# Three edits to a tuned decoder-layer kernel: gate products in runs of four, one projection norm moved a chunk later, one norm broadcast put behind products

## The chip, the cores and the metric

One core of one Trainium2 chip runs the whole layer. The metric is the device time of one execution in microseconds (us); the time of the kernel before is the median of three runs. One further execution was profiled, and every statement about single instructions comes from that one.

## The reference, cut to what matters

The reference is one layer of a hybrid causal decoder, in float32, for a prompt of 2048 tokens and 64 sample tokens (2112 columns in all), with 1024 model features:

```
h    = rmsnorm(x, g_pre_mix)
proj = h @ w_in                # attention q, k, v; GLA q, k, v, r; and a_lr, 16 columns
logf = log_sigmoid(a_lr @ w_a2 + b_a) / 16        # forget gate of the GLA heads
mixed = concat(attention, gated linear attention) @ w_o
x1   = x + rmsnorm(mixed, g_post_mix)
h2   = rmsnorm(x1, g_pre_ffn)
g, u = split(h2 @ w_up)
f    = (gelu(causal_conv3(g)) * u) @ w_down
y    = x1 + rmsnorm(f, g_post_ffn)
```

Every rmsnorm needs, per token, the sum of squares over the 1024 features, its inverse root, and a multiplication of the row by it.

## The kernel before, in words

**Layout.** Features lie on the 128 partitions in 8 tiles (KT = 8), tokens on the free axis. A float32 product is made of three products of rounded parts (high by high, high by low, low by high), so every operand is split into a high part (ScalarE copy, L70) and a low part (a subtraction on VectorE or GpSimd, L73).

**Stages.** `sweeps` makes the input projections chunk by chunk (512 tokens, 576 in the last chunk), first the GLA columns (`sweep_b`, chunks 0 to 3), then the attention columns (`sweep_a`). Attention follows. `tail` then works on four chunks of 528 tokens (H = 264, two halves): the output projection with `w_o` (`wo`, four chunks), and the feed-forward part (`ffn`, four chunks).

**Gate products.** `xhat("b", c)` (L205) loads the 8 input tiles of chunk c into buffers called `raw` (four of them, `rawb=4`), scales each on VectorE (L228), splits it, and multiplies it by the 16 padded-to-32 columns of `a_lr` (`walr`) on TensorE (L247). Each of these products has 32 output rows; product kk goes to the 32 partitions from 32 * (kk % 4) of the PSUM tile `plr`, so four neighbours go to four different column groups of the array. They were issued two at a time, whenever k is odd. A float32 product shows as two records in the trace. A `raw` buffer can be loaded again only when the product and the split that read it are done. The tiles of chunk c + 1 are prepared during the last blocks (`v`) of `sweep_b(c)`: one `next(xg)` per block.

**Norms in the tail.** `rms_bcast` (L116) sums the squares over the partitions with TensorE (`pn`, L126: five small products), takes the inverse root on VectorE and GpSimd (L105, then the power on GpSimd, L107), and after `gap` steps broadcasts the result with five TensorE transposes (`pb`, L143); ScalarE copies it out (L63). `pin=True` puts these TensorE instructions, in TensorE's own order, behind the last product issued so far (`self.after`, L287: an order edge without a semaphore).

`post(c)` (L447) turns the projection of chunk c into the residual stream: first norm; then for each of 8 tiles a scaling (L1459), the addition of x (L1460), the store of `x1` (L1462), and the sum of squares for the next norm (L1278); then the second norm, whose row goes to `rs2` (L1469). It is a generator: each `yield` is one step, and others call it between their products. In `tail` (L1313 to L1330) `post(c)` is stepped while `wo(c + 1)` runs: two steps per output tile for even chunks, three for odd. What is left after `wo(3)`, that is the end of `post(2)` and all of `post(3)`, is the chain `pend` (L1335), which `ffn(0)` steps.

**Feed-forward.** `ffn(c)` (L1618) goes through groups of 4, 4, 4, 4, 2 and 4 blocks of 128 hidden features. For each pair of blocks it runs `strassen` twice (gate half and up half): seven block products of 12 matmuls each (L1583), from four blocks by Strassen's scheme; after the products 1, 3, 5 and 7 one step of `pend` is taken (L1587), after the others one step of `xprep(c + 1)` (L1589). Then `down` (L1598) multiplies the group by `w_down` (L92, tiles `pfd`). Weights come through eight slots `ws`; in chunk 0 they are loaded raw, summed (L1549 to L1552) and split on VectorE and ScalarE (`wsrc`, L1540), and stored for the later chunks, which load four of each seven ready-made (L1558).

The right-hand operands of the seven products are 14 blocks (`xst`) made by `xprep` and loaded by `xload` (L1522) through GpSimd's own DMA queue, two loads of 264 KB per block: product 1 (and 4) reads blocks 0 to 3, product 2 (and 6) blocks 4 to 7, product 3 (and 5) blocks 8 to 11, product 7 blocks 12 and 13.

In `ffn(0)` the steps of `pend` that are left at the end of group 1 are run out (L1669); in the other chunks this happens at the end of group 0, and `pend` is then `final(c - 1)`, the last norm and store of the chunk before.

**Buffers.** `px` (L956) is one ring of four tiles of 264 KB: for x (`bx`), for `x1` in `final` (`fx`), and for the high parts in `xprep` (`xsh`). The projections `mot` of chunk 3 lie in the eight `acc` tiles (L1437) that `ffn(0)` uses for its sums after group 0.

**Order of the work.** The order on each engine and queue is set at build time: a list scheduler with a simulated timeline (`schedule_with_timeline_sim=True`, L1962) takes the instructions as the program issues them, and keeps the edges of `self.after`. Nothing around this change is ordered by hand but by these edges. Loads and stores go through SyncE's queue (SP) unless said otherwise; each queue is worked off in order.

## Time and profile before

| What | Value |
|---|---|
| Median of 3 runs | 2790.16 us (2789.48 to 2796.5) |
| The profiled execution's own time | 2790.49 us |
| Span of the profiled execution, first to last instruction | 2788.7 us |
| TensorE (PE) busy | 2680.4 us, 96% |
| VectorE (DVE) busy | 1829.6 us, 66% |
| ScalarE (ACT) busy | 1268.0 us, 45% |
| GpSimd (POOL) busy | 567.3 us, 20% |
| Mean granted TensorE clock | 0.979 of full speed |

The profile is one execution on the chip. "Busy" counts the time in which an engine has an instruction running; PEld is the load of weights into the array, which runs beside PE. In a table of windows, each row gives the stretch in us from the start of the span, its length, then for each engine the busy time and the number of its instructions in brackets, then the granted clock (PEclk, 1.00 is full speed), the busy share of the DMA engines and the GB/s that they moved. In a timeline, a row gives start, length, engine, line, operation, output and inputs, shape and count, and in brackets how long the engine had been idle and what ended this. In the chain that ended last, a row gives start, length, and the work that carried the chain. In a list of waits, the numbers are the sum in us, the number of waits and the longest.

### The profile page before, as it was taken

How to read it: one execution, taken by the hardware profiler on the slowest of the kernel's cores; microseconds unless marked ns; L12 is line 12 of the kernel's file. 1: busy time of each engine (PE TensorE's matmuls, PEld its weight loads, DVE VectorE, ACT ScalarE, POOL GpSimd, SP SyncE). 2: the span in 40 equal slices, each digit the busy share in tenths (PEclk: the TensorE clock that was granted, in tenths of full speed). 3: DMA queues.
4: the chain of work that ended last, by engine and by line, in shares of the span. 5: the costliest groups of instructions: out<-in, count | busy, mean ns of one | idle time of the engine just before them, and what ended most of it. 6: DMA issues, size and time to landing. Idle time of an engine off the chain costs nothing.

```text
span 2788.7 us, 58335 instructions
## 1 busy us (share of the span) xinstructions
PE 2680.4 (96%) x22203; PEld 2538.7 (91%) x22203; DVE 1829.6 (66%) x4508; ACT 1268.0 (45%) x2959; POOL 567.3 (20%) x626
## 2 busy tenths in 40 slices
PE   8999999999989898998999999999999999999998
PEld 6888899788778787998899999999999999999997
DVE  7557655454347577466989889676577765666666
ACT  6535433333257686344654444534244333443332
POOL 3434242443323567002000011000020000200001
PEclk9999999999999899999999999999999999999998
DMA  8755446789798855368578678886698865976654
GB/s 311 251 182 182 164 136 202 272 327 362 268 204 173 185 155 139 107 211 288 174 283 296 242 259 321 286 301 225 211 330 284 297 238 198 330 258 211 222 187 152
DMA packets 283591, 656.80 MB, mean 236 GB/s; under 512 B 31840, under 2 KB 81632, under 8 KB 281264
## 3 DMA queue, kind: packets, MB, share of 16 engines
q1 hardware_dynamic: 253008, 574.66, 61.2%
q0 software_dynamic: 13216, 46.56, 5.1%
q10 hardware_dynamic: 17088, 31.86, 3.2%
q8 instruction: 175, 2.87, 0.4%
q14 instruction: 104, 0.85, 0.1%
HBM read 509.02 MB, written 143.94 MB: 234 GB/s over the span
## 4 chain that ended last, share of the span: by engine, by line
PE 75%; DMA 9%; DVE 8%; POOL 3%; issue 3%; ACT 1%; SPq 1%; ACTq 0%; DVEq 0%; POOLq 0%
PE pfd L92 17%; PE pv L396 9%; PE pfa L1583 8%; PE pfe L1583 8%; PE pfd L1583 8%; PE pq L92 6%; PE pfb L1583 4%; PE pbo L1424 3%; PE pas L1815 2%; PE pao L1858 2%; PE pat L1841 1%; DVE ws L73 1%; DMA av<-out_o_vp 1%; DMA raw<-in_xp 1%; POOL aop L1222 1%
## 5 line engine op out<-in xcount | busy, mean ns | idle before, releaser
L70 ACT ACTIVATE ws<-wr 128x512 fp32r<-128x512 f32 (+1 forms) x482 | 293.3, 616 | 427.3 <-PE pfe L1583 142.6
L92 PE MATMUL pfd<-hh,ws 128*128 128x264 f32 x2816 | 475.8, 286 | 6.0 <-ACT ws L70 5.0
L92 PEld LDWEIGHTS pfd<-hh,ws 128*128 128x128 f32 x2816 | 401.5, 189 | 8.1 <-ACT ws L70 6.7
L73 DVE TENSOR_TENSOR ws<-wr,ws 128x512 fp32r<-128x512 f32 (+1 forms) x482 | 319.4, 668 | 128.1 <-ACT ws L70 124.1
L92 PE MATMUL pfd<-hl,ws 128*128 128x264 f32 x1408 | 303.5, 285 | 0.0
L1583 PE MATMUL pfa<-xh,ws 128*128 128x264 f32 x1496 | 292.0, 286 | 6.3 <-DVE ws L73 2.9
L1583 PE MATMUL pfe<-xh,ws 128*128 128x264 f32 x1496 | 289.2, 286 | 4.4 <-DVE u L1570 3.0
L1583 PE MATMUL pfd<-xh,ws 128*128 128x264 f32 x1408 | 288.5, 285 | 2.5 <-DVE up L1570 2.5
L1583 PEld LDWEIGHTS pfa<-xh,ws 128*128 128x128 f32 x1496 | 236.9, 190 | 7.8 <-DVE ws L73 3.3
L1583 PEld LDWEIGHTS pfe<-xh,ws 128*128 128x128 f32 x1496 | 236.1, 189 | 5.1 <-DVE u L1570 3.4
L396 PE MATMUL pv<-wh,xh 128*128 128x256 f32 (+1 forms) x816 | 235.2, 288 | 2.3 <-DVE th L693 2.3
L1583 PEld LDWEIGHTS pfd<-xh,ws 128*128 128x128 f32 x1408 | 231.0, 189 | 3.1 <-DVE up L1570 2.9
L396 PE MATMUL pv<-wh,xl 128*128 128x256 f32 (+1 forms) x816 | 233.1, 286 | 0.0
L396 PE MATMUL pv<-wl,xh 128*128 128x256 f32 (+1 forms) x816 | 232.9, 285 | 0.0
L92 PEld LDWEIGHTS pfd<-hl,ws 128*128 128x128 f32 x1408 | 226.5, 189 | 0.1
L1824 ACT ACTIVATE ass<-ass,aml 128x256 f32<-128x256 f32 (+1 forms) x384 | 173.5, 454 | 95.2 <-DVE aml L1820 94.4
L1532 POOL DMA_DIRECT2D xl<-d_xst x52 | 28.1, 540 | 904.5 <-PE pfe L1583 560.1
L1583 PE MATMUL pfd<-xl,ws 128*128 128x264 f32 x704 | 200.7, 285 | 0.0
L92 PE MATMUL pq<-xh,wh 128*128 128x512 f32 (+2 forms) x480 | 174.0, 370 | 10.1 <-ACT xh L234 7.7
L1583 PE MATMUL pfe<-xl,ws 128*128 128x264 f32 x616 | 175.6, 285 | 0.0
L1611 DVE TENSOR_TENSOR acc<-acc,pfd 128x264 f32<-128x264 f32 x304 | 116.2, 422 | 90.5 <-PE pfd L92 90.2
L92 PE MATMUL pq<-xl,wh 128*128 128x512 f32 (+2 forms) x480 | 175.1, 366 | 0.0
(334 smaller groups left out, 6645.2 us busy)
## 6 DMA issues: line engine op xcount, KB each, us to landing
ws<-d_wst SPq DMA_DIRECT2D x248, 512.0 KB
wr<-in_wu SPq DMA_DIRECT2D x114, 512.0 KB
d_wst<-ws SPq DMA_DIRECT2D x88, 512.0 KB
wr<-in_wd SPq DMA_DIRECT2D x160, 256.0 KB
wr<-in_wt SPq DMA_DIRECT2D x60, 512.0 KB
wh<-d_wbs SPq DMA_DIRECT2D x35, 512.0 KB
wl<-d_wbs SPq DMA_DIRECT2D x35, 512.0 KB
skp<-in_ckt SPq DMA_DIRECT2D x16, 1024.0 KB
```

Source lines behind the costliest of these rows:

```text
L70: h = nc.scalar.activation(hi, src, AF.Copy)
L73: return h, (nc.gpsimd if lo_eng == "p" else nc.vector).tensor_tensor(lo, src, hi.bitcast(F32), op=ALU.subtract)
L92: mm = nc.tensor.matmul(o, ww[:, k, :], xx[:, s0:s0 + n], start=(k == order[0] and i == 0), stop=(k == order[-1] and i == 2))
L396: mm = nc.tensor.matmul(ps[:m, :256], x[:, t0:t0 + m], w[:, k % 4, :], start=(k == 0 and i == 0), stop=(k == KT - 1 and i == 2))
L1222: line(nc.gpsimd.tensor_tensor(OP[i][:, :, sl], OP[i][:, :, sl], W[:, i], op=ALU.mult))
L1424: self.lastmm = nc.tensor.matmul(o, ww[:, k, :], xx[:, s0:s0 + n], start=k == self.WORD[0] and i == 0, stop=k == self.WORD[-1] and i == 2)
L1532: self.nc.gpsimd.dma_start(t.bitcast(F32), xo[i, z])
L1583: self.lastmm = nc.tensor.matmul(bank[:, :H], w[:, ww, k, :], xx, start=new and k == 0 and j == 0, stop=k == 3 and j == 2, skip_group_chec ...
L1611: nc.vector.tensor_tensor(acc[m][:, s0:s0 + n], acc[m][:, s0:s0 + n], pz, op=ALU.add)
L1815: self.line(nc.tensor.matmul(ps[:, sc:sc + nk], lq, rk[z], start=(z == 0), stop=(z == 1)))
L1824: ex = nc.scalar.activation(ssb[:, sc:sc + nk], ssb[:, sc:sc + nk], AF.Exp, bias=self.ml[:, idx, h:h + 1], scale=-1.0, accum_out=self.ml[: ...
L1858: self.line(nc.tensor.matmul(po[64 * h:64 * h + 64, blk, :], L.vq[self.base + kb][:, 64 * h:64 * h + 64], pt[:, j, :], start=st, stop=sp))
```

## The change

Three edits, which do not depend on each other:

1. `xhat`: the gate products are issued four at a time, at k = 3 and k = 7, each behind the one before (`self.after`), and, but for chunk 0, the first of a run behind the scaling of the fourth tile (`made`).
2. The norm of chunk 3's projection: `post(3)` is replaced by `post_norm(3)`, which takes the first norm only, stores the unscaled projection into `x1` and the norm's row into `rs2`; and by `post_late(3)`, which becomes `pend` of `ffn(1)` after its group 0. `post_late` loads the row, and for each tile the stored projection and x; it scales, adds, sums the squares, stores `x1` again; then it takes the second norm and stores `rs2` again. `ffn` gets a parameter `more` for it, and what is left of it is run out at the end of the last group.
3. The second norm of `post(2)` has a gap of 9 steps where it had 3. (The first norm of `post(3)` had a gap of 9 and its second one of 5; `post_norm(3)` has 4 and `post_late(3)` has a lead of 6 and a gap of 5.)

```diff
             else:
                 r = p.tile([128, self.W], F32, name=self.n("raw"), tag="raw", bufs=self.rawb)
                 nc.sync.dma_start(r[:, :w], self.a["xp" if ph == "a" else "xn"][:, k, c * 512:c * 512 + w])
-                nc.vector.scalar_tensor_tensor(r[:, :w], r[:, :w], self.gv[:, 0, k:k + 1], rb[:, :w],
-                                               op0=ALU.mult, op1=ALU.mult)
+                made = nc.vector.scalar_tensor_tensor(r[:, :w], r[:, :w], self.gv[:, 0, k:k + 1], rb[:, :w],
+                                                      op0=ALU.mult, op1=ALU.mult)
...
-                if k % 2:
+                if k % 4 == 3:
                     for z, n in ((0, 512), (1, w - 512)):
-                        for kk in (k - 1, k) if n else ():
+                        for kk in range(k - 3, k + 1) if n else ():
                             g = 32 * (kk % 4)
-                            nc.tensor.matmul(plr[g:g + 32, z, :n], walr[:, kk, :], rs[kk][:, 512 * z:512 * z + n],
-                                             start=(kk < 4), stop=(kk >= 4))
+                            mm = nc.tensor.matmul(plr[g:g + 32, z, :n], walr[:, kk, :], rs[kk][:, 512 * z:512 * z + n],
+                                                  start=(kk < 4), stop=(kk >= 4))
+                            if not first:
+                                self.after(mm, made)
+                            made = mm
...
-                    posts.append(self.post(c, self.mot, self.ssq))
+                    posts.append(self.post(c, self.mot, self.ssq) if c < 3 else self.post_norm(c, self.mot, self.ssq))
...
             for c in range(4):
-                pend = self.ffn(c, self.xnext, pend)
+                pend = self.ffn(c, self.xnext, pend, self.post_late(3) if c == 1 else None)
...
-        yield from self.rms(ssq, w, rb, 1, 3 if c < 3 else 9, pin=True)
+        yield from self.rms(ssq, w, rb, 1, 3, pin=True)
...
-        yield from self.rms(ssq2, w, rb2, 2, 3 if c < 3 else 5, pin=True)
+        yield from self.rms(ssq2, w, rb2, 2, 3 if c < 2 else 9, pin=True)
...
+    def post_norm(self, c, mot, ssq):
+        t0 = FCH[c][0]
+        w = 2 * H
+        rb = self.t528("brb", "rb", 2)
+        g = self.rms(ssq, w, rb, 1, 4, pin=True)
+        for m in range(KT):
+            self.nc.sync.dma_start(self.a["x1"][:, m, t0:t0 + w], mot[m])
+            if m % 2:
+                next(g, None)
+                yield
+        for _ in g:
+            yield
+        self.nc.sync.dma_start(self.a["rs2"][:, t0:t0 + w], rb)
+        yield
+
+    def post_late(self, c):
+        nc, a = self.nc, self.a
+        t0 = FCH[c][0]
+        w = 2 * H
+        rb = self.t528("brb", "rb", 2)
+        nc.sync.dma_start(rb, a["rs2"][:, t0:t0 + w])
+        ssq = self.t528("bssq2", "ssq", 2)
+        for m in range(KT):
+            r, o = self.px("bx"), self.px("bo")
+            nc.sync.dma_start(o, a["x1"][:, m, t0:t0 + w])
+            nc.sync.dma_start(r, a["xn"][:, m, t0:t0 + w])
+            yield
+            nc.vector.scalar_tensor_tensor(o, o, self.gv[:, 1, m:m + 1], rb, op0=ALU.mult, op1=ALU.mult)
+            nc.vector.tensor_tensor(o, r, o, op=ALU.add)
+            self.ssq_add(ssq, o, w, m == 0, "v")
+            nc.sync.dma_start(a["x1"][:, m, t0:t0 + w], o)
+            yield
+        rb2 = self.t528("brb", "rb", 2)
+        yield from self.rms(ssq, w, rb2, 6, 5, pin=True)
+        yield
+        nc.sync.dma_start(a["rs2"][:, t0:t0 + w], rb2)
+        yield
...
-            if gi == (c == 0) and pend is not None:
+            last = gi == len(FG) - 1
+            if (last or gi == (c == 0)) and pend is not None:
                 for _ in pend:
                     pass
-                pend = None
-            last = gi == len(FG) - 1
+                pend, more = more, None
```

2 lines of the change are left out of this document (1 added, 1 removed).

## The prediction

> **What bounds the kernel now.** I read the engines' table first, then windows of 50 us over the whole span, then narrower windows, the chain that ended last, and timelines where TensorE falls short.
>
> ```profile
> PE 2680.4 (96%) x22203; PEld 2538.7 (91%) x22203; DVE 1829.6 (66%) x4508; ACT 1268.0 (45%) x2959; POOL 567.3 (20%) x626
> ...
> 1300.00:1350.00 50.00, 40.41 (x316) 40.33 (x315) 40.22 (x80) 26.73 (x51) 9.23 (x12) 0.86 0.49 184
> 1350.00:1400.00 50.00, 43.49 (x316) 42.54 (x315) 47.81 (x90) 28.68 (x56) 0.00 (x0) 0.90 0.68 239
> 1500.00:1550.00 50.00, 47.26 (x383) 46.63 (x383) 45.88 (x94) 24.19 (x44) 0.00 (x0) 1.00 0.81 292
> 1550.00:1600.00 50.00, 50.00 (x415) 50.00 (x414) 44.39 (x91) 26.02 (x45) 0.00 (x0) 1.00 0.60 209
> ```
>
> TensorE is the bound: 96% busy. So an edit pays in two ways only: it makes TensorE's own work shorter, or it removes a stretch in which TensorE falls short. A full window of the feed-forward part holds 415 products of the array in 50 us, 0.1205 us each (1550 to 1600). The two windows after 1300 us, which are the first group of `ffn(0)`, hold 316 each: 99 too few, 12 us each, 24 us together. That is what edits 2 and 3 can work for. It is more than the idle time (9.6 and 6.5 us), because the granted clock fell as well. The narrow windows show two separate holes:
>
> ```profile
> 1304.00:1312.00 8.00, 0.00 (x0) 0.00 (x0) 7.35 (x14) 2.85 (x6) 5.51 (x7) 0.53 1.04 401
> 1312.00:1320.00 8.00, 7.54 (x42) 7.54 (x43) 0.88 (x2) 2.39 (x5) 0.41 (x1) 0.62 0.63 242
> 1344.00:1352.00 8.00, 8.00 (x69) 8.00 (x68) 8.00 (x14) 3.63 (x8) 0.00 (x0) 1.00 0.12 35
> 1352.00:1360.00 8.00, 6.07 (x50) 5.86 (x50) 8.00 (x17) 5.42 (x9) 0.00 (x0) 1.00 0.45 139
> 1360.00:1368.00 8.00, 6.06 (x42) 5.84 (x41) 8.00 (x16) 2.81 (x5) 0.00 (x0) 0.87 1.00 356
> 1368.00:1376.00 8.00, 5.36 (x27) 4.84 (x27) 8.00 (x17) 4.77 (x8) 0.00 (x0) 0.71 0.87 316
> 1376.00:1384.00 8.00, 8.00 (x54) 8.00 (x54) 8.00 (x17) 3.82 (x7) 0.00 (x0) 0.78 0.52 170
> ```
>
> **Edit 3, the broadcast of chunk 2's second norm.** The first hole is one instruction:
>
> ```profile
> 1301.70 1.17 PE L126 MATMUL pn<-c_ones,bssq 128*128 128x1 f32 x10
> ...
> 1309.71 2.71 POOL rcy L107
> 1312.46 1.33 PE pb L143 x5
> 1313.79 2.64 PE pfa L1583 x12
> 1316.43 2.24 PE pfb L1583 x12
> ...
> 1331.48 1.47 PE pfe L1583 x12
> ```
> ```profile
> PE pb L143 <- POOL rcy L107: 9.6, 1, 9.6
> ```
>
> The five transposes `pb` stand ahead of the first product in TensorE's order and wait for GpSimd's power, and GpSimd gets to it only at 1309.71, when it has issued its last load of `xst` blocks. TensorE stands for 9.6 us; then the clock is down, and the first two products take 2.64 and 2.24 us where one takes 1.47 later: 1.9 us more. At stake: 11.5 us.
>
> Counting the steps of `post(2)`, 20 are taken when `wo(3)` ends; with a gap of 9 the transposes come at the 25th. That is the fifth step that `ffn(0)` takes, behind the first strassen and one product more: eight products or so, 12 us. GpSimd's result is there at 1312.4, so it hides behind them. What is late next? Product 3, which reads blocks 8 to 11:
>
> ```profile
> 1296.64 0.54 POOL L1532 DMA_DIRECT2D xh<-d_xst  x1
> ...
> 1304.99 0.54 POOL L1532 DMA_DIRECT2D xl<-d_xst  x1
> ...
> 1297.74 0.44 SPq L1457 DMA_DIRECT2D bx<-in_xn  x1
> ...
> xl<-d_xst POOLq DMA_DIRECT2D x10, 264.0 KB, 7.3
> ...
> 1286.14 0.68 DVE L73 TENSOR_TENSOR ws<-wr,ws 128x512 fp32r<-128x512 f32 x1
> ...
> 1310.67 0.68 DVE L73 TENSOR_TENSOR ws<-wt,ws 128x512 fp32r<-128x512 f32 x1
> ...
> 1319.08 0.69 DVE L1549 TENSOR_TENSOR wt<-wr,wr 128x512 f32<-128x512 f32 x1 [7.73 <-DMA wr<-in_wu]
> ```
>
> The two loads of each block are issued in the order of the blocks; those of block 7 end at 1296.64, those of block 11 at 1304.99, and a load lands about 7.3 us later: 1303.9 and 1312.3. So products 1 and 2, whose split weights were ready by 1286.9, can run from 1302.9 to 1305.8, and product 3 waits until about 1312.3. Of the 11.5 us, 6.5 us of waiting come back, and some of the slow clock. But the four loads of x that `post(3)` makes ahead into the `px` ring go (the last at 1297.74; 1.06 MB, 2.6 us at the 401 GB/s of the window), so the blocks land earlier; and VectorE, which filled the eight weight slots by 1311.4 and then stood 7.7 us, can go on sooner. I take 5.5 us gained; the ends are 1, if weights are late as well, and 11.5, if nothing else is.
>
> **Edit 2 in `ffn(0)`.** In the second hole VectorE is busy 8.00 of 8.00 us in each row from 1344 to 1384. Full rows hold 69; the four after 1352 hold 173 instead of 276, which is 103 x 0.116 = 11.9 us. The work of `post(3)` in that stretch:
>
> ```profile
> L1459 DVE SCALAR_TENSOR_TENSOR bmo<-bmo,c_gvec,brb 128x528 f32<-128x528 f32 x8 | 5.5, 758 | 0.0
> L1460 DVE TENSOR_TENSOR bmo<-bx,bmo 128x528 f32<-128x528 f32 x8 | 5.5, 697 | 0.0
> ...
> L1278 DVE TENSOR_TENSOR bssq<-bssq,sq 128x528 f32<-128x528 f32 x7 | 4.9, 695 | 0.0
> ```
>
> It is 15.9 us of VectorE, more than the hole, and all of it leaves. What is late next is VectorE's other work (sums and splits of weights, evacuations), which fills about 85% of what remains; at such a load the window from 1500 to 1550 (45.88 of 50) still loses 3.9 us, the one from 1550 to 1600 (44.39) nothing. I keep 2 us of loss: 10 us gained, between 6 and 12. What `post_norm` leaves here costs TensorE nothing new: ten records `pn` and five transposes, as before, with GpSimd free of loads by then; the eight stores of `x1` wait only for ScalarE's copies and release the `acc` tiles sooner than the stores after scaling did.
>
> By the Trainium skill (TensorE: Matmul & The Clock Gate, "HAM oscillation"), only idle gaps over about 3.4 us lower the clock. By that rule the second hole, whose rows are idle for 1.9, 1.9 and 2.6 us of 8, would cost its idle 6.5 us alone, and edit 2 would gain about 5 us less. The trace disagrees: the clock went to 0.71 there.
>
> **Edit 1, the gate products.**
>
> ```profile
> 84.00:110.00 26.00, 4.38 (x16) 0.71 (x16) 1.00 0.73 256
> 180.00:206.00 26.00, 5.25 (x16) 0.71 (x16) 1.00 0.67 232
> 276.00:300.00 24.00, 5.69 (x32) 1.63 (x32) 1.00 0.74 262
> ```
> ```profile
> 18.62 1.92 PE L247 MATMUL plr<-raw,walr 128*32 128x512 f32 x16
> ...
> 95.68 1.05 PE L247 MATMUL plr<-raw,g_walr 128*32 128x512 f32 x4
> ...
> 100.87 1.23 PE L247 MATMUL plr<-raw,g_walr 128*32 128x512 f32 x6
> ...
> 107.48 1.04 PE L247 MATMUL plr<-raw,g_walr 128*32 128x512 f32 x2
> ...
> 278.32 1.16 PE L247 MATMUL plr<-raw,g_walr 128*32 128x512 f32 x8
> ```
>
> The windows count this line alone: chunks 1, 2 and 3 spend 15.3 us of TensorE on it. One product (x2) takes 1.04 us, two (x4) 1.05, three (x6) 1.23, all eight in chunk 0 (x16) 1.92: neighbours in different column groups overlap. A run of four is not shown; it lies between 1.05 and 1.92, nearest to the run of three, so I take 1.25, and 1.45 in chunk 3, whose last 64 columns add four short products (two of them made 1.05 into 1.16). Six runs: 4 x 1.25 + 2 x 1.45 = 7.9 us, a saving of 7.4; with 1.92 each it is 3.8. The Trainium skill (TensorEngine Tiling (Array Packing), "Key Properties") says that different tiles run in parallel: then a run of four would cost what one product costs, and the saving would be about 9 us. The run of three at 1.23 says that it is a little less.
>
> Against it: four `raw` buffers are now held until the fourth product, so tiles 4 to 7 can all be loaded only after the first run, where tiles 4 and 5 came earlier.
>
> ```profile
> 104.49 0.75 DVE L228 SCALAR_TENSOR_TENSOR raw<-raw,c_gvec,rb 128x512 f32<-128x512 f32 x1 [1.09 <-DMA raw<-in_xn]
> ```
>
> Tile 7 of chunk 1 was scaled at 104.49 after waiting for its load, and its gate product came at 107.48. TensorE now comes some 2 us sooner and tile 7 does not, and it still has to be split: I charge 0.8 us per chunk, 2.4 in all, and keep 5.0 us gained, between 0 and 8. Chunk 0 has all eight in one stretch already: nothing.
>
> **Edit 2 in `ffn(1)`.** `post_late` adds there what left `ffn(0)`, and eight stores and eight loads that did not exist.
>
> ```profile
> 1780.00:1870.00 90.00, 90.00 (x741) 90.00 (x741) 66.60 (x139) 37.77 (x68) 0.00 (x0) 1.00 0.86 307
> ...
> SPq L1462 <- DVE gt L1570: 12.8, 2, 12.6
> ```
>
> VectorE: 8 x (0.76 + 0.70 + 0.70) = 17.3 us on top of 66.6 in 90 us of groups 1 and 2: 93%. DMA: 24 transfers of 264 KB and two rows, 6.9 MB, 76 GB/s on top of 307: 383, under the 401 of the first hole. The norm's `pn` and `pb` have 10 products and more between them and GpSimd is free. TensorE has no idle time here, so nothing can be gained. The cost lies between 0 (like 1550 to 1600) and 7 us (3.9 us per 50, as in 1500 to 1550); I take 2.
>
> **The sum.** 5.5 + 10 + 5 - 2 = 18.5 us off the profiled execution's 2790.5 us (its span is 2788.7): 2772.0. The median of the runs shown, 2790.16, is the same within 0.4, so I predict 2772 for the median.
>
> **The rivals.** *The first hole stays.* Product 3 waits for its blocks, the clock falls, and by 1320 TensorE is where it was: for it, the loads go on until 1312 to 1316 and the DMA engines are full (share 1.04); against it, two products are surely done earlier. Then 10 + 5 - 2 = 13: 2777.5. *The holes close wholly.* The scheduler puts ready products of the up half into the wait: 10 + 11 + 7 - 1 = 27: 2763.5. *The late tiles eat edit 1.* If tile 7 comes 2.5 us late in each of three chunks, the 7.4 us are gone: 13.5, 2777. *The edges don't hold what they say*, since a list scheduler reorders everything and other stretches shift by chance: half of it, 2781. *Slower: SP's queue.* `post_late` takes two of four `px` tiles per step, `xprep(2)` uses the same ring, and a load that waits for a tile holds every weight load behind it on SP. The profile has such a hold: 12.6 us at a store of `x1` (L1462). The eight weight slots cover 8 x 1.47 = 11.8 us; a hold of 14.1 us in each of eight steps loses the whole gain of edits 1 to 3 (8 x 2.3 = 18.5), and 16 us gives 8 x 4.2 = 34, less 20.5: 2804. Against it: the ring turns in `final(0)` without such holds, and the scheduler places a load where it expects the tile to be free.
>
> **How the numbers follow.** Forecast 0.55 (its own range 2765 to 2779), first hole stays 0.13, holes close 0.12, late tiles 0.08, edges 0.07, slower 0.05. The unknown costs reach from 6 + 1 + 0 - 4 = 3 to 12 + 11.5 + 8 = 31; cut to eight cases in ten: 2762 to 2783. A difference of 0.3%, 8.4 us, is about what a measurement of this kernel can tell from no change. Faster by more than that (under 2781.8): 0.85; within it: 0.10; slower: 0.05.
>
> **What would show it.** Right: no idle time ahead of `pb` near 1302 us, product 1 starting within 1 us of `pn`, an idle of a few us ahead of product 3 named after an `xh` or `xl` load; between 1340 and 1384 rows with 66 or more products and VectorE under 7 of 8; six runs of gate products of 1.2 to 1.5 us after chunk 0; full windows in `ffn(1)` with VectorE near 40 of 50. The first group of `ffn(0)` should end near 1354 us instead of 1374. Wrong: `pb` or another norm still waiting for GpSimd; TensorE in `ffn(1)` waiting for `ws` loads or for VectorE by more than 7 us; TensorE waiting for `xh` or `xl` splits at the start of chunks 1 to 3.

## The result, and the profile after

Timed beside the kernel before on the same chip, the changed kernel takes 2780.7 us in the median of 8 runs (2776.14 to 2786.49), the kernel before 2793.42 us (8 runs, 2788.44 to 2800.43). The ratio is 0.9956, with a 95% interval of 0.9944 to 0.9968. On the 2790.16 us of the prediction that is 2777.9 us, with 2774.5 and 2781.2 as ends: faster by 12.3 us where 18.5 were forecast, inside the range. The profiled execution took 2780.57 us, with a span of 2778.5 us, 10.2 us less than the span before.

The table of engines, then windows of 50 us (start and end, length, busy time and count for each engine, clock, DMA share, GB/s), after the change. Line numbers from here on are the changed kernel's: the products of `strassen` are L1624, VectorE's evacuations L1611.

```profile
PE 2669.0 (96%) x22203; PEld 2530.5 (91%) x22203; DVE 1827.3 (66%) x4508; ACT 1271.4 (46%) x2961; POOL 568.2 (20%) x626
```
```profile
1300.00:1350.00 50.00, 44.65 (x344) 43.88 (x343) 45.11 (x89) 29.39 (x52) 3.41 (x3) 0.93 0.48 170
1350.00:1400.00 50.00, 50.00 (x412) 50.00 (x412) 40.33 (x76) 27.72 (x57) 0.00 (x0) 1.00 0.69 244
1500.00:1550.00 50.00, 50.00 (x412) 50.00 (x411) 45.86 (x92) 26.27 (x46) 0.00 (x0) 1.00 0.67 236
1550.00:1600.00 50.00, 50.00 (x414) 50.00 (x413) 40.41 (x84) 22.53 (x41) 0.00 (x0) 1.00 0.56 196
1780.00:1870.00 90.00, 89.09 (x731) 88.69 (x730) 70.79 (x150) 39.50 (x74) 1.56 (x1) 1.00 0.93 338
```

The two windows after 1300 held 316 products each; they hold 344 and 412. The window of `ffn(1)` held 741 and holds 731: something was paid there. The narrow rows and TensorE's waits between 1290 and 1330 show what became of the two holes.

```profile
1312.00:1320.00 8.00, 3.88 (x32) 3.66 (x30) 8.00 (x17) 6.19 (x10) 0.00 (x0) 0.95 0.37 112
1320.00:1328.00 8.00, 7.03 (x40) 7.03 (x41) 6.91 (x14) 2.55 (x4) 0.00 (x0) 0.63 0.28 97
...
1344.00:1352.00 8.00, 8.00 (x67) 8.00 (x67) 6.21 (x12) 3.95 (x8) 0.00 (x0) 1.00 0.82 301
1352.00:1360.00 8.00, 8.00 (x68) 8.00 (x67) 6.96 (x15) 4.54 (x9) 0.00 (x0) 1.00 0.66 194
1360.00:1368.00 8.00, 8.00 (x68) 8.00 (x67) 6.34 (x12) 5.87 (x13) 0.00 (x0) 1.00 0.64 211
```
```profile
1294.94 1.17 PE L126 MATMUL pn<-c_ones,bssq 128*128 128x1 f32 x10
1295.97 1.71 PE L1624 MATMUL pfa<-xh,ws 128*128 128x264 f32 x12
...
1299.68 0.52 PE L1624 MATMUL pfe<-xh,ws 128*128 128x264 f32 x2 [0.55 <-ACT ws L70]
...
1300.15 1.62 PE L1624 MATMUL pfa<-xh,ws 128*128 128x264 f32 x12
...
1302.22 0.28 PE L1624 MATMUL pfa<-xh,ws 128*128 128x264 f32 x1
```
```profile
PE pfe L1624 <- DVE u L1611: 5.4, 2, 5.1
```
```profile
1319.12 0.36 ACT L1615 COPY u<-pfa 128x264 f32<-128x264 f32 x1
```

The wait of `pb` is gone: the first product starts right behind `pn`. Behind products 1 and 2 (`pfa`, `pfb`) TensorE waits 0.55 us at the start of product 4 (`pfe`, which reads blocks 0 to 3), for ScalarE's split of its weights and not for blocks of x. Product 3 does not come next: the scheduler put product 1 of the up half (`pfa`, 1300.15) ahead of it, and product 3 (`pfa` from 1302.22, between pieces of products 4 and 5) waits for nothing. The second hole is gone altogether. But a new wait of 5.1 us stands in the first group, up to 1320.97, for an evacuation `u` that VectorE has to do; VectorE is busy 8.00 of 8.00 us in that row, so it lies behind other work in VectorE's queue, and the clock is at 0.63 in the row after. One input of that evacuation was late as well: ScalarE's copy of the up half's product 3 (the last row) ended at 1319.48. VectorE's queue alone accounts for the 1.0 us from there to 1320.50, where the evacuation starts.

The gate products (L247 alone) after the change, by window and as rows of the timeline:

```profile
84.00:110.00 26.00, 2.75 (x16) 0.45 (x16) 1.00 0.76 259
180.00:206.00 26.00, 2.79 (x16) 0.45 (x16) 1.00 0.68 229
274.00:300.00 26.00, 3.39 (x32) 0.94 (x32) 1.00 0.62 215
```
```profile
92.75 1.06 PE L247 MATMUL plr<-raw,g_walr 128*32 128x512 f32 x8
...
104.61 1.69 PE L247 MATMUL plr<-raw,g_walr 128*32 128x512 f32 x8
```
```profile
104.44 0.75 DVE L228 SCALAR_TENSOR_TENSOR raw<-raw,c_gvec,rb 128x512 f32<-128x512 f32 x1 [1.11 <-DMA raw<-in_xn]
```

15.3 us of TensorE have become 8.9. In the second run of chunk 1 three products start within 0.02 us and the fourth 0.64 us later, at 105.25, when VectorE's scaling of its tile (the last row), which had waited for a load, has ended; in chunk 2 it is 0.68 us.

**Where the time went, by stages.** All traces hold the same TensorE instructions apart from those of the norms (`pn`, `pb`), which the change moves. Without these each trace has 21957, so the time at which the Nth of them starts can be compared from kernel to kernel. Each number below is the us between two such starts, read from the traces of all thirteen kernels and of the kernel before; the experiments are described in the next section.

```
TensorE instruction    0-380 -1700 -2760 -10305 -11000 -11850 -13450 -16250 -21900  end
                       start  GLA1  GLA2  attn   ffn0a  ffn0b  ffn0c   ffn1   rest  
before                  76.1 175.9 123.4  922.0  113.1  109.4  200.3  347.8  697.6 23.2
gap_only                77.6 175.8 124.8  923.4   99.8  119.7  201.7  348.8  697.9 23.9
norm_only               73.9 176.0 121.8  919.1  101.3  110.7  200.2  356.3  700.0 23.8
no_gates                74.4 175.9 121.8  924.7   97.0  108.2  201.0  354.5  698.1 23.7
gates_only              77.1 174.3 125.5  916.9  110.8  110.2  200.5  349.7  698.1 22.9
after                   74.3 174.6 124.7  916.9   97.5  113.4  199.7  356.3  698.1 23.0
gates_422               76.3 177.5 122.2  918.7   97.7  108.7  201.1  355.8  699.8 23.2
no_late                 76.6 173.5 125.2  916.8   99.1  110.0  201.0  350.5  697.8 23.5
late_ahead              75.8 173.8 125.3  919.6   97.2  108.5  199.2  353.9  700.1 23.4
late_g3                 76.8 173.2 125.9  916.8   97.8  111.0  200.2  353.4  698.9 23.5
store_shift             73.9 173.6 125.7  919.2   98.3  110.0  199.7  362.9  697.9 23.8
xa_behind               74.4 172.9 123.0  917.5   98.3  111.6  200.8  357.6  699.4 23.3
late_g3_xa              76.9 173.1 123.4  918.8   96.7  112.0  200.5  353.0  698.0 22.8
all_three               73.9 173.4 123.2  917.3   97.3  110.0  201.5  362.3  698.5 23.1
```

GLA1 is the linear attention up to the middle of its last chunk but one, GLA2 the rest of it; "attn" is everything from there to the end of `wo`; ffn0a holds both holes. After less before, column by column and rounded at the end: -1.7, -1.2, +1.3, -5.1, -15.6, +4.0, -0.6, +8.5, +0.5, -0.2, together -10.2. The start (0 to 380) lies between 73.9 and 77.6 us over kernels that share its code, so its -1.7 is nothing. The rest has four parts: the two feed-forward holes gave 15.6; the gate products gave nothing inside the linear attention; 5.1 came from a stage that the diff does not touch; and 12.5 were paid back, in ffn0b and `ffn(1)`. There is one trace of each kernel, and a single column is no safer than this: in "attn" norm_only and no_gates have the same instructions in the same order on every engine and on SP, and take 919.1 and 924.7 us. The traced execution of gap_only is 8.9 us above that kernel's median; the others lie within about 4 us of theirs.

### The profile page after: what moved, and what is told of

It is laid out like the page before. It is cut to its first block, busy times and chain, and to the rows that moved or that the text cites. A ratio compares the mean times of both kernels' runs of the same rounds, so it can differ in the third digit from the quotient of the medians.

```text
span 2778.5 us, 58351 instructions
## 1 busy us (share of the span) xinstructions
PE 2669.0 (96%) x22203; PEld 2530.5 (91%) x22203; DVE 1827.3 (66%) x4508; ACT 1271.4 (46%) x2961; POOL 568.2 (20%) x626
## 4 chain that ended last, share of the span: by engine, by line
PE 78%; DMA 9%; DVE 6%; POOL 2%; issue 2%; ACT 2%; SPq 0%; ACTq 0%; DVEq 0%; POOLq 0%
PE pfd L92 17%; PE pv L399 9%; PE pfe L1624 8%; PE pfd L1624 8%; PE pfa L1624 8%; PE pbo L1427 7%; PE pq L92 6%; PE pfb L1624 4%; PE pas L1856 2%; DMA av<-out_o_vp 2%; DMA ws<-d_wst 2%; PE pao L1899 1%; PE pat L1882 1%; DMA raw<-in_xp 1%; DMA akl<-d_kl 1%
## 5 line engine op out<-in xcount | busy, mean ns | idle before, releaser
L1624 PE MATMUL pfe<-xh,ws 128*128 128x264 f32 x1496 | 291.5, 287 | 9.5 <-DVE u L1611 5.9
L1624 PE MATMUL pfa<-xh,ws 128*128 128x264 f32 x1496 | 290.0, 285 | 4.6 <-ACT ws L70 1.9
L1624 PE MATMUL pfd<-xh,ws 128*128 128x264 f32 x1408 | 290.8, 286 | 1.8 <-DMA ws<-d_wst 1.0
L1624 PEld LDWEIGHTS pfe<-xh,ws 128*128 128x128 f32 x1496 | 237.4, 190 | 11.3 <-DVE u L1611 7.0
L1624 PEld LDWEIGHTS pfa<-xh,ws 128*128 128x128 f32 x1496 | 235.3, 188 | 5.9 <-ACT ws L70 2.4
L1624 PEld LDWEIGHTS pfd<-xh,ws 128*128 128x128 f32 x1408 | 232.5, 190 | 2.6 <-DVE ws L73 1.4
L1624 PE MATMUL pfd<-xl,ws 128*128 128x264 f32 x704 | 201.2, 286 | 0.0
L92 PE MATMUL pq<-xh,wh 128*128 128x512 f32 (+2 forms) x480 | 171.3, 366 | 10.3 <-ACT xh L234 7.8
L1624 PE MATMUL pfe<-xl,ws 128*128 128x264 f32 x616 | 176.3, 286 | 0.0
L1624 PE MATMUL pfa<-xl,ws 128*128 128x264 f32 x616 | 174.9, 284 | 0.0
```

What stands on the lines that cost most here:

```text
L92: mm = nc.tensor.matmul(o, ww[:, k, :], xx[:, s0:s0 + n], start=(k == order[0] and i == 0), stop=(k == order[-1] and i == 2))
L1624: self.lastmm = nc.tensor.matmul(bank[:, :H], w[:, ww, k, :], xx, start=new and k == 0 and j == 0, stop=k == 3 and j == 2, skip_group_chec ...
```

## The experiments

My theories, the last of them formed after the first eight runs: (a) edit 1's saving is lost where the last chunk's decay runs, because four held `raw` buffers put late loads ahead of it in VectorE's queue; (b) the moved norm costs `ffn(1)` more than 2 us because its steps wait in in-order queues there; (c) the rest of the repayment is traffic on full DMA engines. Rivals: (a') the wait for `gS` comes from the decay's own length; (b') the work costs the same anywhere; (c') the queues and engines, not the traffic.

### The parts alone

**gates_only**, edit 1 alone on the kernel before:

```diff
-                if k % 2:
+                if k % 4 == 3:
...
-                        for kk in (k - 1, k) if n else ():
+                        for kk in range(k - 3, k + 1) if n else ():
...
+                            if not first:
+                                self.after(mm, made)
...
```


> Edit 1 alone: gate products in runs of four, everything else as before. In the profile of the changed kernel the gate products take 8.9 us of TensorE instead of 15.3, but at the end of the GLA stage only 1.7 us are left of these 6.4. Theory: in each chunk TensorE gets to the state products pgo earlier and waits there for VectorE's state update gS, which is queued behind the decay chain; the chain's end is set by loads into the raw buffers, which are now held until the fourth product. It expects 1 to 3 us faster than before (ratio 0.9990 to 0.9996), and in the trace the same wait of about 4 us of pgo for gS in chunk 3. Rival: the gain is real and was lost elsewhere in the changed kernel by chance of the schedule; it expects 5 to 6.4 us faster (ratio near 0.998).

Measured: 2788.83 us (12 runs, 2779.88 to 2802.4), before 2794.04 (25 runs); ratio 0.9983 (0.9969 to 0.9998). That is 4.7 us (0.6 to 8.6), nearer to the rival than to the theory, but the interval holds both. The trace has what the theory says: the linear attention is no shorter than before (299.7 us against 299.2), and `pgo` waits 4.2 us for `gS` in chunk 3.

**gap_only**, edit 3 alone:

```diff
-        yield from self.rms(ssq2, w, rb2, 2, 3 if c < 3 else 5, pin=True)
+        yield from self.rms(ssq2, w, rb2, 2, (3, 3, 9, 5)[c], pin=True)
```


> Edit 3 alone: the third chunk's second norm has a gap of 9 steps, the last chunk's norm stays where it was. Theory A, separate holes: the wait of 9.6 us for GpSimd goes, a shorter wait for VectorE or for loaded blocks comes, 3 to 6 us faster (ratio about 0.9985). Theory B, VectorE's work is what ends the first group of the first feed-forward chunk: TensorE runs ahead, meets the full VectorE earlier, and the second hole grows by what the first lost: within 2 us of before.

Measured: 2786.42 us (12 runs, 2778.69 to 2798.98); ratio 0.9979 (0.9964 to 0.9994): 5.9 us, the size of theory A. The trace, below, has theory B's second hole.

**norm_only**, edit 2 alone:

```diff
-                    posts.append(self.post(c, self.mot, self.ssq))
+                    posts.append(self.post(c, self.mot, self.ssq) if c < 3 else self.post_norm(c, self.mot, self.ssq))
...
-                pend = self.ffn(c, self.xnext, pend)
+                pend = self.ffn(c, self.xnext, pend, self.post_late(3) if c == 1 else None)
```


> Edit 2 alone: chunk 3's projection norm moved into the second feed-forward chunk; the gap of the third chunk's second norm stays at 3, so its broadcast stands ahead of the first product. Theory A, two separate holes: the second hole (about 12 us, VectorE full with the moved work) closes and the first (9.6 us of waiting for GpSimd) stays, less 4 to 7 us that the second chunk and the end of the first give back: 4 to 8 us faster, ratio about 0.998. Theory B, the two holes are one, because VectorE's work is what ends the first group: without edit 3 VectorE stands still while TensorE waits, and edit 2 alone still gains nearly all: 9 to 11 us faster.

Measured: 2783.29 us (7 runs, 2777.31 to 2786.94); ratio 0.996 (0.9946 to 0.9974): 11.2 us, the size of theory B. Its trace has theory A's mechanism: the first hole stays in full, and the second all but goes (TensorE is busy for 38.8 of the 40 us from 1340).

```profile
PE pb L143 <- POOL rcy L107: 9.6, 1, 9.6
```

**no_gates**, edits 2 and 3 without edit 1:

```diff
-                if k % 4 == 3:
+                if k % 2:
...
```


> Edits 2 and 3 without edit 1: the gate products again in pairs, the norm moved and the broadcast put back as in the changed kernel. Theory (the edits do not depend on each other, and edit 1 is worth 1.7 us): 8.5 to 11 us faster than before, ratio about 0.9965, and both holes after the end of the output projection closed as in the changed kernel: 14 us gained by the end of the first group of the first feed-forward chunk, and 5 to 7 us given back afterwards. Rival (edit 1 carries most of the measured gain, also through the attention, where the changed kernel's trace is 5 us shorter without any change of the program): 4 to 6 us faster.

Measured: 2779.85 us (6 runs, 2777.13 to 2788.28); ratio 0.9952 (0.9934 to 0.997): 13.4 us, more than both forecasts name, though the interval reaches down to 8.4. 16.1 us go out of ffn0a, where 14 were expected, and 6.2 come back by the end of `ffn(1)`, as expected.

What follows. The ratios of the single parts add up to more than the whole (4.7, 5.9 and 11.2 us against 12.3), each known to about 4 us; by stages, edits 2 and 3 give more together than apart. In its trace edit 3 alone takes 13.3 us out of ffn0a and gives 10.3 back in ffn0b: windows of gap_only show the second hole, only later.

```profile
1406.00:1416.00 10.00, 7.39 (x61) 7.18 (x59) 10.00 (x19) 6.00 (x13) 0.00 (x0) 1.00 0.97 352
1416.00:1426.00 10.00, 7.50 (x42) 7.51 (x43) 9.80 (x21) 4.59 (x8) 0.00 (x0) 0.66 0.74 282
```

VectorE is full there (10.00 and 9.80 of 10) with `post(3)`, which is still in its way. Edit 2 alone takes 11.8 out of ffn0a and returns 1.3; both together 16.1 and nothing returned. So edit 2 carries the gain of the first feed-forward chunk, and edit 3 adds 6.8 us to it over the two columns, where alone it keeps 3.0. And no_gates, without edit 1, is as fast as the whole change.

### What became of edit 1

In the columns GLA1 and GLA2 the kernels with runs of four and the decay's order as written (gates_only, after, no_late, late_ahead, late_g3, store_shift) take 173.8 and 125.4 us in the mean, the four without edit 1 take 175.9 and 122.9: 2.1 us gained, then 2.4 lost. The products of chunks 1 and 2 save 4.1 us, so half of that is gone within GLA1: TensorE's waits for VectorE from 72 to 252 us sum up to 3.6 us before and 7.0 after. The last chunk shows where the rest goes. TensorE's waits from 300 to 335 us, before and after:

```profile
PE pgo L827 <- DVE gS L836: 2.7, 1, 2.7
```
```profile
PE pgo L843 <- DVE gS L839: 4.0, 1, 4.0
```

TensorE comes earlier and waits longer for `gS`. VectorE's timeline after the change, on the way to it, with the product that the decay needs from TensorE and the loads from SP:

```profile
301.04 1.88 PE L630 MATMUL pz<-lr,g_wa 128*128 128x512 f32 x4
```
```profile
297.91 1.28 SPq L227 DMA_DIRECT2D raw<-in_xp  x3
```
```profile
302.74 1.55 DVE L228 SCALAR_TENSOR_TENSOR raw<-raw,c_gvec,rbp 128x576 f32<-128x576 f32 x2 [7.46 <-DMA raw<-in_xp]
...
305.72 1.40 DVE L631 TENSOR_SCALAR lfm<-pz,g_ba 128x512 f32<-128x512 f32 x2
...
313.16 0.34 DVE L632 SCALAR_TENSOR_TENSOR gB<-lfm,pz 128x64 f32<-128x64 f32 x2
```

VectorE stood idle for 7.5 us at the first scaling of the next phase's blocks, which waited for a load. SP issued that at 297.91, at the end of the second run of four, which held the buffers; before the change the first two went out at 292.68:

```profile
292.68 1.30 SPq L227 DMA_DIRECT2D raw<-in_xp  x2
```

`lfm`, whose products on TensorE began at 301.04, comes behind these scalings in VectorE's queue, at 305.72. The kernel before has scalings ahead of `lfm` too, with 2.9 and 1.0 us of waiting for loads, but there `lfm` starts 0.6 us after its product is done (304.23 after 303.68), and here 3.7 us (305.72 after 302.06).

**xa_behind**: the same kernel, with these scalings put behind the decay.

```diff
+                if ph == "a" and c == 3:
+                    self.after(made, self.lastdec)
...
-                nc.vector.scalar_tensor_tensor(t[:, sl], m[:, sl], 2.0, pzz, op0=ALU.mult, op1=ALU.subtract)
+                self.lastdec = nc.vector.scalar_tensor_tensor(t[:, sl], m[:, sl], 2.0, pzz, op0=ALU.mult, op1=ALU.subtract)
```


> The changed kernel with one order added: in the last chunk of the linear attention, VectorE's first touches of the next phase's input blocks come behind the last step of the decay (gB from pz). Theory: edit 1's saving is given back in the last chunk because the raw blocks held for the runs of four load late and stand ahead of the decay in VectorE's in-order queue; then the decay's lfm, which came 2.8 us after its product was done, comes 3 to 4 us earlier, PE's wait of 4.0 us for gS falls below 1.5 us, the linear attention ends 2 to 4 us earlier than in the changed kernel, and the whole is 2 to 4 us below it (about 2777.5). Rival: gS is late for another reason (the decay's own length, the PE work that now arrives sooner): the wait stays within 1 us of 4.0, and the time is the changed kernel's within 1.5 us.

```profile
300.48 0.75 DVE L633 TENSOR_SCALAR lfm<-pz,g_ba 128x512 f32<-128x512 f32 x1 [6.78 <-PE pz L632]
...
306.74 0.22 DVE L634 SCALAR_TENSOR_TENSOR gB<-lfm,pz 128x64 f32<-128x64 f32 x1
306.88 4.17 DVE L228 SCALAR_TENSOR_TENSOR raw<-raw,c_gvec,rbp 128x576 f32<-128x576 f32 x4
```

Measured: `lfm` comes 5.2 us and the last `gB` 6.4 us earlier (1.6 us of that is an earlier arrival at the stage), and the idle time ahead of `lfm` is now ended by TensorE (`pz`). The wait of 4.0 us is two of 2.3 and 1.4, in sum as long as the rival has it. GLA2 takes 123.0 us instead of 124.7, and the whole linear attention (380 to 2760) 295.9, 296.5 and 296.6 us in the three kernels with this order, against 298.8 to 299.7 in the six without it: 2.9 us in the mean, where 2 to 4 were expected. 2.2 of them lie in GLA2, which comes to 123.2 us in the mean, near the 122.9 of the kernels without edit 1. So theory (a) holds for the loss in the last chunk. No run has this order without edit 1, so how much the order alone would win there is open. The whole takes 2781.25 us (6 runs), ratio 0.9958 (0.9941 to 0.9974): nothing of it is left at the end, against what I expected.

**gates_422**: the last four products of a chunk in two runs of two.

```diff
-                if k % 4 == 3:
+                if k in (3, 5, 7):
...
-                        for kk in range(k - 3, k + 1) if n else ():
+                        for kk in range(0 if k == 3 else k - 1, k + 1) if n else ():
```


> The changed kernel with gate products in runs of four, two and two per chunk instead of four and four. Theory: holding four blocks until the last run delays the next loads; with the last four released two by two the loads of the last chunk's next phase issue about 3 to 5 us earlier, the wait for gS shrinks by 1 to 2 us, against about 1 us more per chunk for one run more on TensorE (gate products 8.9 to about 12 us in the three chunks): the linear attention ends within 1 us of the changed kernel's and the whole is the same within 1.5 us. Rival: the runs' cost alone decides, and it ends 2 to 3 us later.

Measured: 2783.45 us (6 runs), ratio 0.9966 (0.9952 to 0.9979). The gate products of chunks 1 to 3 take 15.6 us, as much as before: behind the first run of four they ran one at a time (in chunk 1 at 99.67, 100.72, 107.64 and 109.28), where I had expected two runs of two and about 12 us. GLA1 takes 177.5 and GLA2 122.2, 299.6 together, as in the changed kernel (299.3): the buffers come free earlier, the wait falls to 1.5 us, and the products' own time eats that. By the stage the theory's end holds; by the whole, 2.8 us above the changed kernel, its rival, but the two intervals overlap.

**What edit 1 did elsewhere.** The column "attn" is 916.8 to 919.6 us in the ten kernels with any form of edit 1 (mean 917.9) and 919.1 to 924.7 in the four without it (mean 922.3): 4.4 us, in a stage for which the diff has no line. The order of the instructions differs there all the same: between the kernel before and gates_only, 81 places of 7620 on TensorE (the first at 952 us), 54 of 1563 on VectorE and 44 of 1268 on ScalarE hold another instruction, while gap_only's order is the same as before's. So edit 1 shifts the order that the list scheduler chooses much later. That this order is the cause of the 4.4 us is not shown. Single executions of one order differ as much: norm_only and no_gates by 5.6 us over the stage, and gap_only spends 34.1 us between instructions 7260 and 7510 (919 to 945 us in the kernel before) where before spends 26.2.

### The moved norm in `ffn(1)`

**no_late**: `post_late` not run.

```diff
-                pend = self.ffn(c, self.xnext, pend, self.post_late(3) if c == 1 else None)
+                pend = self.ffn(c, self.xnext, pend, None)
```


> The changed kernel without the part of edit 2 that runs in the second feed-forward chunk: the last chunk's second norm is left out (its x1 stays unscaled, without the residual, and its rs2 is the first norm's). Theory: the moved steps cost 4 to 7 us there, since their loads and stores stand in queues that the down weights and the products' sums use; without them the wait for weights of about 4.6 us near the start of the steps goes, and the whole is 4 to 7 us below the changed kernel (about 2775). Rival: those waits are the round trips of weights that the kernel before has there too; then no more than 1.5 us is gained.

Measured: 2775.3 us (6 runs, 2774.0 to 2781.97), ratio 0.994 (0.9927 to 0.9952). `ffn(1)` takes 350.5 us instead of 356.3: the moved steps cost 5.8 us, sure to about 2 us, since the four other kernels with the same steps in this place (norm_only, no_gates, gates_422 and xa_behind) take 354.5 to 357.6. 1.9 of the 5.8 us are the norm's own products on TensorE:

```profile
1832.50 1.17 PE L126 MATMUL pn<-c_ones,bssq 128*128 128x1 f32 x10
...
1847.05 0.71 PE L143 MATMUL pb<-c_ident,rcy 128*128 128x128 f32 x5
```

The size is the theory's, the place is not: the wait near 1712 to 1742 stays. Windows of no_late, then of the changed kernel:

```profile
1712.00:1742.00 30.00, 24.51 (x181) 23.50 (x179) 25.69 (x51) 12.10 (x21) 0.00 (x0) 0.94 0.80 264
```
```profile
1712.00:1742.00 30.00, 24.08 (x164) 22.81 (x164) 24.71 (x48) 10.40 (x18) 0.00 (x0) 0.89 0.84 296
1742.00:1832.00 90.00, 90.00 (x741) 90.00 (x740) 71.08 (x145) 44.04 (x87) 0.00 (x0) 1.00 0.90 331
1832.00:1877.00 45.00, 44.09 (x362) 43.69 (x361) 33.95 (x71) 19.86 (x38) 1.56 (x1) 1.00 0.88 315
```

5.5 us of TensorE are idle in the first row with the steps left out, 5.9 with them; with them the clock is lower as well, and 17 products fewer are done. The longest wait of that hole, 2.1 us, is for a stored weight, at the seam of the two chunks; the kernel before has such a hole too, with 4.3 us idle from 1732 to 1762 (no_late's `ffn(1)` is 2.7 us longer than before's). Followed from product to product, the 5.8 us lie in three places: 1.9 at this seam; 3.1 between instructions 14350 and 14750, which are the norm's own 1.9 and a wait of 0.9 for a stored weight; and 0.9 in the last hundred instructions. The seam is no safe witness, since late_g3, whose steps begin later, loses 0.7 us there against no_late.

**late_ahead**: the loads of each block six steps ahead of its arithmetic instead of one, over twice as many steps.

```diff
-        for m in range(KT):
+        def fetch(m):
             r, o = self.px("bx"), self.px("bo")
...
+            return r, o
+
+        nxt = fetch(0)
+        yield
+        for m in range(KT):
+            r, o = nxt
+            if m < KT - 1:
+                nxt = fetch(m + 1)
+            yield
             yield
...
+            yield
             yield
```


> The changed kernel with the moved norm in the second feed-forward chunk spread out: each block's two loads are issued six steps ahead of its arithmetic instead of one, and the eight blocks take twice as many steps. Nothing is left out. Theory: what the moved steps cost is waiting for their own loads in the in-order queues of VectorE and SP (6.1 us of waits for bo); spaced out, most of the 4.6 us near their start comes back and the whole is 2 to 5 us below the changed kernel. Rival: the cost is the traffic and VectorE work itself, which are the same here: the time is the changed kernel's within 1.5 us, the waits only move.

Measured: 2780.75 us (6 runs), ratio 0.9956 (0.9941 to 0.997), the changed kernel's. The waits for `bo` fall from 6.1 to 2.0 us, but those for `bx` rise from 2.0 to 4.6; `ffn(1)` takes 353.9, 2.4 less. By the whole the rival is right, by the stage half of the theory.

**late_g3**: the moved norm begins behind the third group of `ffn(1)` instead of the first.

```diff
-                pend, more = more, None
+                pend = None
+            if gi == 2 and more is not None:
+                pend, more = more, None
```


> The changed kernel with the last chunk's second norm begun two groups later in the second feed-forward chunk: behind its third group instead of its first, where the trace of the changed kernel has 193 GB/s on the DMA engines (1892 to 1982) instead of 402 GB/s (1772 to 1802). Nothing is left out. Theory: the 4 to 5 us that leaving these steps out won are the price of their place among full DMA engines and a full VectorE; begun later they cost below 1.5 us, and the whole is 2 to 5 us below the changed kernel (ratio to before about 0.994). Rival: their VectorE work and the norm's broadcast cost the same anywhere: within 1.5 us of the changed kernel.

```profile
1742.00:1832.00 90.00, 90.00 (x742) 90.00 (x741) 57.40 (x119) 38.51 (x76) 0.00 (x0) 1.00 0.79 274
1832.00:1877.00 45.00, 45.00 (x372) 45.00 (x371) 38.57 (x77) 22.07 (x40) 0.00 (x0) 1.00 0.97 348
1877.00:1922.00 45.00, 45.00 (x371) 45.00 (x370) 33.65 (x70) 17.91 (x33) 0.00 (x0) 1.00 0.98 363
```

Measured: 2779.33 us (7 runs, 2770.79 to 2785.59), ratio 0.9957 (0.994 to 0.9973). In the stage the theory holds: 353.4 us, 2.9 above no_late, of which 1.9 are the norm's own products, so 1.0 us of waits is left of 3.9, 0.7 of it at the seam, before the steps begin; late_g3_xa, below, takes 353.0. The row 1832 to 1877 has its 372 products again. But the DMA engines are full in the new place as well (0.98, 363 GB/s) and TensorE is not held up there (45.00 of 45): full DMA engines alone are not the price. The whole does not show the 2.9 us; it lies inside the interval, so the 2 to 5 us expected of it are not shown.

### The traffic

**store_shift**: the weight sums of tiles 8 to 11 stored by the second chunk instead of the first.

```diff
-        cs = int(f < 4)
+        cs = int(f < 4 or 8 <= f < 12)
```

As the line taken out shows, the first four tiles were stored by the second chunk already.

> The changed kernel with one rule of the feed-forward weights altered: the sums of up-projection weights of tiles 8 to 11 are stored for the later chunks by the second chunk instead of the first (8.4 MB less to write in the first chunk; the second computes these sums again). Nothing is left out. Theory: what the closed holes gained is partly given back in the first feed-forward chunk because its DMA engines are full there (share 0.82 to 1.00 and 306 to 373 GB/s from 1446 to 1496): the 6.8 us that TensorE idles between 1416 and 1426 and between 1476 and 1496 shrink to below 3, the rows there fall to a DMA share below 0.9, and the whole is 2 to 5 us below the changed kernel. Rival: the idle time is VectorE's and ScalarE's work on the weights that come in late by the order of the queues, not by traffic: it stays within 1.5 us, and the added sums in the second chunk cost 0 to 3 us.

Windows of the changed kernel, then of store_shift:

```profile
1446.00:1476.00 30.00, 30.00 (x249) 30.00 (x248) 27.84 (x54) 13.57 (x26) 0.00 (x0) 1.00 0.94 336
1476.00:1496.00 20.00, 15.54 (x112) 14.71 (x111) 18.56 (x40) 11.87 (x24) 0.00 (x0) 0.93 0.93 343
```
```profile
1446.00:1476.00 30.00, 30.00 (x250) 30.00 (x248) 29.27 (x58) 13.79 (x26) 0.00 (x0) 1.00 0.46 143
1476.00:1496.00 20.00, 18.23 (x148) 17.80 (x147) 19.77 (x42) 12.56 (x23) 0.00 (x0) 1.00 0.79 286
...
1832.00:1877.00 45.00, 39.76 (x313) 39.37 (x313) 36.98 (x74) 19.39 (x37) 2.15 (x1) 0.96 0.95 351
```

Measured: 2790.91 us (12 runs), ratio 0.9991 (0.9977 to 1.0005). The traffic from 1446 to 1476 falls from 336 to 143 GB/s and the idle time behind it from 4.5 to 1.8 us; that from 1416 to 1426 stays at 2.3, so 4.0 us are left of the 6.8, where I had expected less than 3. Yet ffn0b takes 110.0 us, and kernels whose traffic is the changed kernel's take 108.2 to 113.4 in the same column. So the writes account for no more than the 3.4 us by which the changed kernel's own trace stands out, and for nothing beside late_ahead or gates_422. Theory (c) is not confirmed. What is plain is the price at the other end: the sums and stores cost `ffn(1)` 6.6 us (362.9 against 356.3), where I had written 0 to 3; by the ratios the whole is 9.8 us above the changed kernel.

**all_three**: xa_behind, late_ahead and store_shift in one kernel (the three diffs above).

> The changed kernel with three alterations together: the decay's order of the last linear-attention chunk, the spaced-out norm of the second feed-forward chunk and the stores of tiles 8 to 11 moved to the second chunk. Nothing is left out. Theory: the 3.4 us that the first one won in the linear attention and that were lost again by the end are no longer swallowed where the DMA engines are full, so the whole is 4 to 8 us below the changed kernel (about 2774). Rival: the feed-forward chunks have a pace of their own set by VectorE and the remaining traffic, so that an earlier arrival is worth nothing at the end: within 2 us of the store change alone.

Measured: 2783.53 us (10 runs), ratio 0.9965 (0.9951 to 0.998). Both expectations miss: its ratio is above the changed kernel's, though not clear of its interval, and its median is 7.4 us below store_shift's.

**late_g3_xa**: the later norm and the decay's order.

> The same later norm, with the decay's order of the last linear-attention chunk as well. Nothing is left out. Theory: what the order wins in the linear attention (3.4 us) was lost where DMA engines are full; with the norm moved out of that stretch half of it stays at the end: 3 to 7 us below the changed kernel (ratio about 0.9935). Rival: the first chunk's full DMA engines swallow it: the same as the later norm alone within 1.5 us.

Measured: 2777.21 us (6 runs, 2770.92 to 2778.09), ratio 0.9947 (0.9932 to 0.9962). It is the fastest complete kernel here, but its interval overlaps the changed kernel's (0.9944 to 0.9968): better by 2 to 3 us is likely, and not shown. The same holds for the 2.8 us between its ratio and late_g3's, of which the rival had allowed 1.5.

## Why the prediction was right, and which terms were wrong

**The holes (5.5 + 10 = 15.5 us forecast): 15.6 in the trace**, 16.1 in no_gates. The reading was right that `pb` held up the first hole and that VectorE's work for `post(3)` was the second. norm_only, in which the first hole stays and the second all but goes, shows them to be two. The working inside was not right. Product 3 was to wait for blocks 8 to 11 until about 1312; in the trace it waits for nothing, since the scheduler ran product 1 of the up half and the start of product 4 ahead of it, as the rival "The holes close wholly" has it. The blocks came sooner as well: the last load of block 11 is issued 2.5 us behind the start of `pn`, where it was 3.3 before, and a load lands in 6.5 us instead of 7.3; which of the two decided is open. What is late next is an evacuation: 5.1 us, in the first group, behind VectorE's queue and ScalarE's late copy. And the 2 us that I kept back for the second hole were not needed.

**Edit 1 (7.4 saved, 2.4 charged, 5.0 kept).** This step failed. TensorE's saving was well priced (6.4 us in the changed kernel's trace). The charge was too small, and only in part in the right place. Tile 7 does come late, by 0.64 and 0.68 us in chunks 1 and 2, but that is inside the 1.69 and 1.73 us of the runs. What took the saving are TensorE's longer waits for VectorE (3.4 us more up to 252 us) and the next phase's blocks ahead of the last chunk's decay: the linear attention is no shorter with edit 1 (299.2 us against 298.8 in the mean). The rival that the late tiles eat edit 1 was right in the outcome, by another mechanism for the most part. Alone, edit 1 gives 0.9983 (0.9969 to 0.9998); on top of edits 2 and 3 (0.9956 against 0.9952) nothing that these runs can tell.

I had put the run of four at 1.25 us, above the one product's 1.04, and had named 1.2 to 1.5 us as a sign of being right; none of the six runs lies there. The three first runs took 1.06, 1.06 and 1.18 us (in the last chunk with its short products), the second ones 1.69 and 1.73, and in the last chunk the fourth product came apart from the other three. The Trainium skill (TensorEngine Tiling (Array Packing), "Key Properties") says that different tiles run in parallel; the first run of a chunk agrees, at 1.06 us for four, and so do the first three products of the second, whose fourth waited for its tile.

**Edit 2 in `ffn(1)` (2 us forecast, 0 to 7).** Mis-sized: 5.8 us, more than the 4 that the low end of the whole sum allows. 1.9 of them are the norm's own products, which I had hidden behind other products although TensorE has no idle time in that stage, as the prediction itself said; 3.9 are waits, and the 353.4 and 353.0 us of the two kernels with later steps show that most of these, some 3 us, depend on where the steps begin.

**What the sum lacked.** Stages behind the holes returned 4.0 us in ffn0b and, apart from `post_late`, 2.7 in `ffn(1)`. Both repayments vary from kernel to kernel with the same code there (108.2 to 113.4 us in ffn0b), and kernels that come to 10305 late tend to make up part of it: from there to 11850 gates_422, late_ahead and no_gates, which come at 1294.4 to 1296.8, take 205.2 to 206.4 us; after, xa_behind, no_late, late_g3 and late_g3_xa, at 1287.8 to 1292.7, take 208.7 to 210.9. TensorE's wait behind the third group's products names one link, ScalarE's split of down weights, which itself waited for a store from its slot:

```profile
1492.81 0.51 PE L92 MATMUL pfd<-hh,ws 128*128 128x264 f32 x2 [2.64 <-ACT ws L70]
```
```profile
1492.13 0.63 ACT L70 ACTIVATE ws<-wr 128x512 fp32r<-128x512 f32 x1 [3.40 <-DMA d_wst<-ws]
```

In store_shift, without those stores, TensorE's wait there is 1.1 us instead of 2.6, but late_ahead, with them, has 1.5. What sets the pace of `ffn(0)` behind its first two groups stays open. So does the time of the attention, above.

So the sum was 6 to 8 us too hopeful. The repayment is the missing term: 12.5 us where 2 were charged. In the trace, 5.1 us from the attention and 1.7 from the start stand against it, which no term had priced and no run shows to be the change's own; that the traced executions lie as far apart as 10.2 us is luck to that extent. The median ratios, from 8 runs each, do not rest on it. For edits 2 and 3 without edit 1 the terms say 13.5 us and no_gates measured 13.4 (8.4 to 18.4), a width that leaves room for all of the misses above.

## What to carry to other kernels

An instruction made shorter gains only up to the next wait of its stage: read what ends that wait, and whether the edit holds a buffer whose next load stands in an in-order queue ahead of it. Work moved into a stage where TensorE is full costs at least its own TensorE time there, and a place in the queue; try the place, not only the move. And where several variants share a stage's code, put their traces side by side by stage: that showed a saving that was lost again before its stage ended, and gains (2 to 3 us) that the timing of the whole cannot tell. But learn first how far two traces of one order differ: here it was 5.6 us in a stage of 920.

## What the runs showed of the hardware

The clock falls after shorter idle stretches than I would have thought. At the seam of the chunks, three waits of 1.23, 1.16 and 2.10 us within 8 us were enough for 0.50; each of these rows is of the changed kernel.

```profile
1715.94 0.39 PE L1624 MATMUL pfa<-xh,ws 128*128 128x264 f32 x1 [1.23 <-ACT ws L70]
1719.06 0.51 PE L1624 MATMUL pfa<-xh,ws 128*128 128x264 f32 x2 [1.16 <-DVE ws L73]
1722.64 0.59 PE L1624 MATMUL pfe<-xh,ws 128*128 128x264 f32 x1 [2.10 <-DMA ws<-d_wst]
```
```profile
1720.00:1724.00 4.00, 1.90 (x11) 1.69 (x10) 3.77 (x8) 1.02 (x2) 0.00 (x0) 0.74 1.03 406
1724.00:1728.00 4.00, 4.00 (x20) 4.00 (x20) 1.79 (x4) 1.16 (x2) 0.00 (x0) 0.50 1.05 405
```

TensorE is busy for all of the last row and gets 20 instructions done, where at the pace of a full window (415 in 50 us) it would be 33. The Trainium skill (TensorE: Matmul & The Clock Gate, "HAM oscillation") names idle gaps of more than about 3.4 us; no single gap here is that long, so the measurement differs, as it did at the second hole of the kernel before, with waits of 1.9 us each.
